# The first 90 microseconds of a decoder layer, reordered: second memory tile, gain row, keys, idle products

## Chip, cores and metric

The kernel runs on one core of a Trainium2 chip. The metric is the device time of one execution, in microseconds. TensorE is called PE, VectorE DVE, ScalarE ACT, GpSimd POOL; SyncE (SP) issues the transfers.

## The reference

One decoder layer on 1024 tokens of width 1024, with 256 memory tokens, everything in float32:

```python
h = rms_norm(x, g_pre_mix);  proj = h @ w_in           # q, k, v, conv gates, qx
q, k = apply_rope(q), apply_rope(k)
y_attn = dilated_mixture_attention(q, k, v)             # 8 heads x 64
y_conv = short_gated_conv(...)
mem_kv = rms_norm(mem, g_mem) @ w_mem_kv                # keys, values of 256 memory tokens
y_x = memory_cross_attention(qx, mem_kv)                # 4 heads x 64
y = concat(rms_norm(y_attn), rms_norm(y_conv), rms_norm(y_x)) @ w_out
x = x + rms_norm(y, g_post_mix)
f = square(relu(rms_norm(x, g_pre_mlp) @ w_up)) @ w_down
x = x + rms_norm(f, g_post_mlp)
```

## The kernel before

Float32 products are made of fp32r parts. `split` copies a value to a high part on ACT (`copy`, L88) and subtracts it for a low part on DVE (`lo_part`, L92). `mm3` (L101 to L103) adds high·high, high·low and low·high into one PSUM bank.

The opening stage stands in one block whose order on ACT, DVE, POOL and PE is written out by hand; SP's order, and all work outside such blocks, is left to a planner. Every engine works through its own queue in order. The stage does the following.

- The memory's gain row (`m_row`) is split on DVE (`spread_row`, L354, L355) and spread over 128 partitions by two products with a row of ones (L357, L358).
- Two memory tiles (`XT[NS]`, `XT[NS+1]`) are squared and summed (`x_sums`, L149 on ACT, L127 on DVE), their reciprocal roots taken on POOL (L130), scaled (`m_norm`, L152), turned by PE (`x_turn`, L304) and split into `mt_h`, `mt_l`.
- The memory weights are cut into parts by `m_cut(k)` into columns of `hh` and `hl` that the tokens need later; ACT makes the high part, and DVE and POOL make the low parts in turn (L364).
- `v_mem(t, k0, k1)` adds the values of memory tile t into a bank, `v_out` takes them out. `k_mem(pr, k0, k1)` and `k_out(pr)` do so for the keys of head pair pr; the keys use the two `mm` banks, which the query products `raw_mms` use after them. `k_out` makes high parts (`KM`), low parts on DVE, and shifted copies (`KMS`).
- The row of `g_pre_mix` is spread by one float32 product per half (`p_spread`, L669), and copied from its bank to `g_tok[0]`.
- Eight token tiles in the order 7 to 0 are squared, normed (`x_norm`, L152), turned and split into `hh`, `hl`. `raw_mms(n, k0)` makes q, k, v of head group 0 for tile n, two of eight chunks at a time. Its weights are cut by `cut` (ACT, L88) and `low` (DVE and POOL in turn, L232).
- `tables` computes the angles in small DVE steps, placed by `table_steps`. `rope0(m)` rotates tile m's q and k on DVE or POOL (L402 to L409). `turn0(c)` turns two tiles by PE (L635) and splits them into `QK` and shifted copies `KS`. The three `qk` tiles are used in rotation, so rope m+3 waits for the turn that reads rope m.
- The weights of head group 1 (`wj1`) are cut in four pairs; the first three projection steps of that group (`steps13`) run in the block, and attention (`pair_windows`) follows.

Of the kernel before, what the change touches and what calls it, by code (L numbers as in the profile page):

```python
# [9 lines left out]
F = mybir.dt.float32  # L10
R = mybir.dt.float32r
# [10 lines left out]
NS = S // 128  # L22
# [23 lines left out]
def hybrid_block(ctx, tc, x, mem, positions, g_pre_mix, g_mem, w_in, w_mem_kv, conv_w, g_attn_out,  # L46
                 g_conv_out, g_xattn_out, w_out, g_post_mix, g_pre_mlp, w_up, w_down, g_post_mlp,
                 ident_in, bias_in, invf_in, out):
    nc = tc.nc
# [22 lines left out]
    def mm_bank(cols=512):  # L72
        return bank("mm", 2, cols)
# [10 lines left out]
    def tp_bank():  # L84
        return bank("tp", 1)

    def copy(o, i, scale=1.0):
        nc.scalar.activation(o, i, AF.Copy, scale=scale)  # L88
# [28 lines left out]
    def rstd(ss, width):  # L117

        n = ss.shape[1]
        ms = small.tile([128, n], F, name="ms", tag="ms")  # L120
        widths = width if isinstance(width, (list, tuple)) else [width] * n
        i = 0
        while i < n:
            k = i
            while k < n and widths[k] == widths[i]:
                k += 1
            nc.vector.tensor_scalar(ms[:, i:k], ss[:, i:k], 1.0 / widths[i], EPS, op0=OP.mult, op1=OP.add)  # L127
            i = k
        r = small.tile([128, n], F, name="rstd", tag="rstd")
        nc.gpsimd.tensor_tensor(r, ms, half_neg.to_broadcast([128, n]), op=OP.pow)  # L130
        return r
# [65 lines left out]
    def load_x(n):  # L197
        XT[n] = stage(name="xt")
        nc.sync.dma_start(XT[n], tokens[n])
# [91 lines left out]
    def x_sums(n):  # L291

        ss = small.tile([128, 1], F, name="ss", tag="ss")
        sumsq(ss, XT[n], 1024)
        RS[n] = rstd(ss, D)

    def x_norm(n):
        norm_to(XT[n], XT[n], g_tok[n // NS], RS[n])

    def x_turn(n, q):  # L300
        t = pt_bank()
        for i in range(4):
            k = 4 * q + i
            nc.tensor.transpose(t[:, i * 128:(i + 1) * 128], XT[n][:, k * 128:(k + 1) * 128], ident)  # L304
        v = t.rearrange("p (k s) -> p k s", k=4)
        if n < NS:
            cl = slice(order[n] * 128, (order[n] + 1) * 128)
            split(hh[:, 4 * q:4 * q + 4, cl], hl[:, 4 * q:4 * q + 4, cl], v)
        else:
            if n == NS:  # L310
                mt_h.append(kv.tile([128, 4, 256], R, name="mth", tag="QK", bufs=NSETS))
                mt_l.append(kv.tile([128, 4, 256], R, name="mtl", tag="QK", bufs=NSETS))
            cl = slice((n - NS) * 128, (n - NS + 1) * 128)
            split(mt_h[q][:, :, cl], mt_l[q][:, :, cl], v)

    RS = {}
    p_row = [kv.tile([128, 512], F, name="g_row", tag="KS", bufs=NSETS) for _ in range(2)]
    for q in range(2):
        nc.scalar.dma_start(p_row[q][:1], g_pre_mix[:, q * 512:(q + 1) * 512])
# [31 lines left out]
    def spread_row(row):  # L351

        hi, lo = (kv.tile([128, 512], R, name="row" + n, tag="V", bufs=NSETS) for n in "hl")
        nc.vector.tensor_copy(hi[:1], row)  # L354
        nc.vector.tensor_sub(lo[:1], row, hi[:1].bitcast(F))  # L355
        b = s_bank()
        nc.tensor.matmul(b, ones[:1], hi[:1], start=True, stop=False)  # L357
        nc.tensor.matmul(b, ones[:1], lo[:1], start=False, stop=True)  # L358
        return b

    def m_cut(k):

        copy(hh[:, k, :512], MW[k])
        (nc.gpsimd if k % 2 else nc.vector).tensor_sub(hl[:, k, :512], MW[k], hh[:, k, :512].bitcast(F))  # L364

    def v_mem(t, k0, k1):
        if k0 == 0:
            MB["v", t] = (ot_bank, tp_bank)[t]()
        for k in range(k0, k1):
            cl = slice(t * 128, (t + 1) * 128)  # L370
            mm3(MB["v", t][:, :256], mt_h[k // 4][:, k % 4, cl], mt_l[k // 4][:, k % 4, cl], hh[:, k, 256:512],
                hl[:, k, 256:512], k == 0, k == KT - 1)
    def v_out(t):
            vm = kv.tile([128, 4, 128], R, name="VM", tag="VM", bufs=2)
            split(vm[:, :, 0:64], vm[:, :, 64:128], MB["v", t][:, :256].rearrange("p (h e) -> p h e", h=4))
            VM.append(vm)
# [261 lines left out]
    def table_steps(n):  # L638
        for _ in range(n):
            next(tab, None)  # L640

    with tc.manual_schedule(engines={ACT, DVE, POOL, PE}):
        def cut(n=1):
            for _ in range(n):
                cuts.pop(0)()

        def low(n=1):
            for _ in range(n):
                lows.pop(0)()

        nc.vector.memset(extra[:1, :128], 1.0)
        nc.vector.tensor_copy(ones[:1], extra[:1, :128])
        gb = [spread_row(m_row[:1, :512])]
        ss = small.tile([128, 2], F, name="ss2", tag="ss2")
        for q in range(2):
            sumsq(ss[:, q:q + 1], XT[NS][:, q * 512:(q + 1) * 512], 512)
        s1 = small.tile([128, 1], F, name="s1", tag="s1")
        nc.vector.tensor_add(s1, ss[:, 0:1], ss[:, 1:2])
        r = rstd(s1, D)
        gb.append(spread_row(m_row[:1, 512:]))  # L660

        def m_norm(n, r):
            for q in range(2):
                cl = slice(q * 512, (q + 1) * 512)
                norm_to(XT[n][:, cl], XT[n][:, cl], gb[q], r)

        def p_spread(q):
            b = mm_bank()
            nc.tensor.matmul(b, extra[:1, :128], p_row[q][:1], start=True, stop=True)  # L669
            return b  # L670
        m_norm(NS, r)
        m_cut(0)
        m_cut(1)
        x_turn(NS, 0)
        x_turn(NS, 1)
        m_cut(2)
        v_mem(0, 0, 2)
        pb = [p_spread(0)]
        m_cut(3)
        v_mem(0, 2, 4)  # L680
        pb.append(p_spread(1))
        x_sums(NS + 1)
        m_cut(4)
        m_norm(NS + 1, RS[NS + 1])
        m_cut(5)
        m_cut(6)
        m_cut(7)
        v_mem(0, 4, 6)
        x_turn(NS + 1, 0)
        x_turn(NS + 1, 1)  # L690
        v_mem(0, 6, 8)
        load_x(3)
        load_x(4)
        g_tok[0] = ac.tile([128, S], F, name="g_pre", tag="bias")
        for q in range(2):
            copy(g_tok[0][:, q * 512:(q + 1) * 512], pb[q])
        x_sums(0)
        cut(2)
        low(2)
        v_out(0)  # L700
        v_mem(1, 0, 8)
        tab = tables()
        x_norm(0)
        table_steps(1)
        k_mem(0, 0, 8)
        v_out(1)
        x_turn(0, 0)
        cut(2)
        low(2)
        x_turn(0, 1)  # L710
        x_sums(1)
        k_mem(1, 0, 4)
        cut(2)
        low(2)
        k_out(0)
        k_mem(1, 4, 8)
        x_norm(1)
        cut(2)
        low(2)
        raw_mms(0, 0)  # L720
        k_out(1)
        x_sums(2)
        table_steps(1)
        raw_mms(0, 2)
        x_turn(1, 0)
        x_norm(2)
        raw_mms(0, 4)
        x_turn(1, 1)
        table_steps(4)
        x_sums(3)  # L730
        raw_mms(0, 6)
        for n in range(1, NS):
            if n + 4 < NS:
                load_x(n + 4)
            if n == 5:
                cuts = []
                wj1 = load_w_in(1, later=cuts, engines=[nc.vector])
            if n == NS - 1:
                bias = ac.tile([128, S], F, name="bias", tag="bias")
                nc.sync.dma_start(bias, bias_in)  # L740
            raw_mms(n, 0)
            if n + 1 < NS:
                x_turn(n + 1, 0)
            else:
                cut(2)
            table_steps(2)
            if n == 5:
                for o in (sin, cos):
                    nc.scalar.activation(o, o, AF.Sin, scale=TWO_PI)
            raw_mms(n, 2)  # L750
            if n + 1 < NS:
                x_turn(n + 1, 1)
            else:
                cut(2)
            if n + 2 < NS:
                x_norm(n + 2)
            if n == 4:
                reduces[0]()
            table_steps(2)
            raw_mms(n, 4)  # L760
            if n + 3 < NS:
                x_sums(n + 3)
            table_steps(2)
            for m in {5: (0, 1), 6: (2, 3), 7: (4, 5, 6)}.get(n, ()):
                rope0(m)
            if n == NS - 1:
                cut(2)
            raw_mms(n, 6)
            if n >= 6:
                turn0(9 - n)  # L770
        turn0(1)
        rope0(7, nc.vector)
        cut(2)
        steps13, turn13 = proj_steps(1, 3, wj1)
        run(steps13[:3])
        turn0(0)
# [901 lines left out]
```

## Time and profile before

| | us |
|---|---|
| median of 3 runs | 1160.62 |
| lowest, highest run | 1157.08, 1161.08 |
| profiled execution | 1158.95 |
| its span | 1157.2 |

The span is the time between the first and the last instruction in the trace; the execution's own time holds 1.75 us more. Times in the rows below are counted from the span's start. An engine's idle time before an instruction is put down to what released it last.

### The profile page before, as it was taken

Reading aid. Unit: us, or ns where it says so; the run is one execution under the profiler, and the core shown is the slowest. Engines: PE = TensorE matmul, PEld = TensorE weight load, DVE = VectorE, ACT = ScalarE, POOL = GpSimd, SP = SyncE. Lnnn points to the kernel's source line nnn. Section 1 sums busy time; section 2 is a strip of 40 time slices with the busy share of each in tenths; the row PEclk is TensorE's granted clock in tenths of the full one; section 3 lists DMA queues with packets and bytes.
Section 4 is the critical chain, followed back from the end, with each engine's and each line's share of the span. In section 5 each row is a group of like instructions: output and inputs, shape, how many; then the busy total and the mean of one; then the engine's idle time right before and its main releaser. Section 6 shows DMA issues by size and latency. Waiting matters only on the chain.

```text
span 1157.2 us, 15949 instructions
## 1 busy us (share of the span) xinstructions
PE 1126.8 (97%) x5785; PEld 961.0 (83%) x5785; DVE 787.5 (68%) x1422; ACT 631.1 (55%) x1202; POOL 82.9 (7%) x107
## 2 busy tenths in 40 slices
PE   8989999999999999999999999999999999999997
PEld 6888989898888878888788888888888888888886
DVE  5888777676757547676876656665695565865776
ACT  5667675666657345655665555555564433433551
POOL 3230020202002021110000000000000000000001
PEclk9999999999999999999999999999999999999999
DMA  8230020100020264333365444544885466432216
GB/s 261 80 100 19 10 61 10 51 5 10 24 74 19 72 198 168 123 133 113 107 197 184 147 137 147 171 146 152 293 298 184 134 220 227 168 105 91 93 36 218
DMA packets 118790, 144.27 MB, mean 125 GB/s; under 512 B 7468, under 2 KB 71604, under 8 KB 118711
## 3 DMA queue, kind: packets, MB, share of 16 engines
q1 hardware_dynamic: 118706, 143.25, 37.6%
q8 instruction: 45, 0.74, 0.3%
q14 instruction: 35, 0.28, 0.1%
q10 hardware_dynamic: 4, 0.00, 0.0%
HBM read 101.28 MB, written 41.94 MB: 124 GB/s over the span
## 4 chain that ended last, share of the span: by engine, by line
PE 85%; DVE 6%; ACT 4%; DMA 2%; issue 1%; POOL 0%; SPq 0%; DVEq 0%; POOLq 0%; ACTq 0%
PE pt L1559 7%; PE sc L1559 7%; PE mm L1559 7%; PE mm L101 6%; PE mm L103 6%; PE mm L102 5%; PE tp L1559 3%; PE ot L1559 3%; PE sc L1263 2%; PE sc L1264 2%; PE sc L1262 2%; PE pt L565 2%; PE mm L1262 2%; PE mm L1264 2%; PE mm L1263 2%; PE sc L500 2%
## 5 line engine op out<-in xcount | busy, mean ns | idle before, releaser
L88 ACT ACTIVATE op<-fraw 128x1024 fp32r<-128x1024 f32 x56 | 59.4, 1060 | 142.2 <-PE tp L1559 72.5
L92 DVE TENSOR_TENSOR op<-fraw,op 128x1024 fp32r<-128x1024 f32 x56 | 68.5, 1224 | 89.3 <-ACT op L88 87.5
L101 PE MATMUL mm<-wh,hh 128*128 128x384 f32 x256 | 91.3, 357 | 4.1 <-DVE KM L92 2.2
L103 PE MATMUL mm<-wh,hl 128*128 128x384 f32 x256 | 87.5, 342 | 0.0
L102 PE MATMUL mm<-wl,hh 128*128 128x384 f32 x256 | 87.3, 341 | 0.0
L1559 PE MATMUL pt<-op 128*128 128x512 f32 x336 | 80.7, 389 | 0.0
L1559 PE MATMUL mm<-op 128*128 128x512 f32 x336 | 80.4, 389 | 0.0
L1559 PE MATMUL sc<-op 128*128 128x512 f32 x336 | 80.4, 389 | 0.0
L1559 PEld LDWEIGHTS pt<-op 128*128 128x128 f32 x336 | 63.1, 188 | 13.1
L1559 PEld LDWEIGHTS mm<-op 128*128 128x128 f32 x336 | 63.1, 188 | 13.1
L1559 PEld LDWEIGHTS sc<-op 128*128 128x128 f32 x336 | 63.1, 188 | 13.1
L92 DVE TENSOR_TENSOR tl<-pt,th 128x512 fp32r<-128x512 f32 (+1 forms) x96 | 59.8, 642 | 13.7 <-ACT th L88 12.8
L92 DVE TENSOR_TENSOR op<-r_b,op 128x1024 fp32r<-128x1024 f32 x56 | 68.3, 1219 | 0.6 <-ACT op L88 0.6
L554 ACT ACTIVATE P<-P,m 128x896 f32<-128x896 f32 (+3 forms) x64 | 49.7, 776 | 30.4 <-DVE m L552 29.7
L1246 ACT ACTIVATE ef<-ef 128x512 f32<-128x512 f32 x48 | 30.3, 631 | 60.4 <-DVE ef L1285 36.0
L144 POOL TENSOR_TENSOR rstd<-ms,half_neg 128x1 f32<-128x1 f32 x24 | 13.5, 561 | 679.7 <-DVE ms L142 679.7
L88 ACT ACTIVATE th<-pt 128x512 fp32r<-128x512 f32 (+1 forms) x96 | 52.1, 560 | 15.0 <-PE pt L565 13.2
L88 ACT ACTIVATE op<-r_b 128x1024 fp32r<-128x1024 f32 x56 | 58.5, 1045 | 3.2 <-issue 3.2
L232 POOL TENSOR_TENSOR wl<-wraw,wh 128x384 fp32r<-128x384 f32 (+1 forms) x40 | 37.4, 963 | 299.4 <-ACT wh L88 253.8
L101 PEld LDWEIGHTS mm<-wh,hh 128*128 128x128 f32 x256 | 49.0, 191 | 4.6 <-issue 2.4
L101 PE MATMUL mm<-hh,wh 128*128 128x512 f32 x128 | 51.9, 405 | 0.0
L103 PE MATMUL mm<-hh,wl 128*128 128x512 f32 x128 | 50.9, 398 | 0.0
(389 smaller groups left out, 3112.3 us busy)
## 6 DMA issues: line engine op xcount, KB each, us to landing
wuraw<-in_w_up SPq DMA_DIRECT2D x32, 512.0 KB, 4.7
f_s<-ef SPq DMA_DIRECT2D x64, 256.0 KB, 2.1
r_b<-in_w_down SPq DMA_DIRECT2D x32, 512.0 KB, 4.8
fraw<-f_s SPq DMA_DIRECT2D x32, 512.0 KB, 3.7
f_a<-ef SPq DMA_DIRECT2D x48, 256.0 KB, 4.0
fraw<-f_a SPq DMA_DIRECT2D x24, 512.0 KB, 4.0
wraw<-in_w_in SPq DMA_DIRECT2D x24, 192.0 KB, 2.7
xt<-in_x SPq DMA_DIRECT2D x8, 512.0 KB, 5.4
```

The lines of the kernel that those rows point to most:

```text
L88: nc.scalar.activation(o, i, AF.Copy, scale=scale)
L92: nc.vector.tensor_sub(lo, src, hi.bitcast(F))
L101: nc.tensor.matmul(o, a_hi, b_hi, start=first, stop=False)
L102: nc.tensor.matmul(o, a_hi, b_lo, start=False, stop=False)
L103: nc.tensor.matmul(o, a_lo, b_hi, start=False, stop=last)
L232: eng.tensor_sub(wt[1][:, :cols], rv[:, k], wt[0][:, :cols].bitcast(F))
L554: nc.scalar.activation(p[:, :nk], p[:, :nk], AF.Exp, scale=-1.0, bias=m, accum_out=den[:, 2 * i + h:2 * i + h + 1])
L1246: nc.scalar.activation(t, t if src is None else src, AF.Relu)
L1262: nc.tensor.matmul(b, w[:, 0, k], th[:, k], start=(k == 0 and not prev), stop=False, skip_group_check=True)
L1263: nc.tensor.matmul(b, w[:, 0, k], tl[:, k], start=False, stop=False, skip_group_check=True)
L1264: nc.tensor.matmul(b, w[:, 1, k], th[:, k], start=False, stop=(k == 3), skip_group_check=True)
L1559: nc.tensor.matmul(b, x[:, k, cl], y[:, k], start=(fresh and s == 0 and k == 0 and m == 0), stop=(s == NSUB - 1 and k == 1 and m == 2), sk ...
```

## The change

A tile of zeros (`zr`) is made on DVE at the start, and `keep` issues products on it into a bank that nothing reads: seven before the first spread row, five between the two, two after them. The second memory tile's square, norm and turn are placed ahead of most of the first tile's value products. The row of `g_pre_mix` is split and spread as the memory's row is, around the first half of the second tile's value products, and the first token tile is normed from the banks. The first keys are taken out before the first token tile is turned; the cuts of the query weights are spread over later places. In the loop over tiles, rope 5 runs on DVE instead of POOL, rope 4 runs one tile earlier, and the last cut of head group 1's weights runs ahead of the turns.

```diff
+    zero = kv.tile([128, 384], F, name="zero", tag="V", bufs=NSETS)
+    zr = kv.tile([128, 384], R, name="zr", tag="V", bufs=NSETS)
+    nc.vector.memset(zero, 0.0)
+    nc.vector.tensor_copy(zr, zero)
+    def keep(src, n, cols=384):
+        b = tp_bank()
+        for _ in range(n):
+            nc.tensor.matmul(b[:, :cols], src[:, :128], src[:, :cols], start=True, stop=True)
...
+        keep(zr, 7)
         gb = [spread_row(m_row[:1, :512])]
...
         r = rstd(s1, D)
+        keep(zr, 5)
         gb.append(spread_row(m_row[:1, 512:]))
...
-        def p_spread(q):
-            b = mm_bank()
-            nc.tensor.matmul(b, extra[:1, :128], p_row[q][:1], start=True, stop=True)
-            return b
+        keep(zr, 2)
         m_norm(NS, r)
         m_cut(0)
         m_cut(1)
         x_turn(NS, 0)
         x_turn(NS, 1)
         m_cut(2)
+        x_sums(NS + 1)
+        m_cut(3)
         v_mem(0, 0, 2)
-        pb = [p_spread(0)]
-        m_cut(3)
+        m_norm(NS + 1, RS[NS + 1])
+        m_cut(4)
+        m_cut(5)
         v_mem(0, 2, 4)
-        pb.append(p_spread(1))
-        x_sums(NS + 1)
-        m_cut(4)
-        m_norm(NS + 1, RS[NS + 1])
-        m_cut(5)
         m_cut(6)
         m_cut(7)
-        v_mem(0, 4, 6)
         x_turn(NS + 1, 0)
         x_turn(NS + 1, 1)
-        v_mem(0, 6, 8)
+        x_sums(0)
+        v_mem(0, 4, 8)
         load_x(3)
         load_x(4)
+        pb = [spread_row(p_row[0][:1])]
+        v_mem(1, 0, 4)
+        pb.append(spread_row(p_row[1][:1]))
+        v_mem(1, 4, 8)
+        v_out(0)
         g_tok[0] = ac.tile([128, S], F, name="g_pre", tag="bias")
         for q in range(2):
-            copy(g_tok[0][:, q * 512:(q + 1) * 512], pb[q])
-        x_sums(0)
-        cut(2)
-        low(2)
-        v_out(0)
-        v_mem(1, 0, 8)
-        tab = tables()
-        x_norm(0)
-        table_steps(1)
+            cl = slice(q * 512, (q + 1) * 512)
+            copy(g_tok[0][:, cl], pb[q])
+            norm_to(XT[0][:, cl], XT[0][:, cl], pb[q], RS[0])
         k_mem(0, 0, 8)
         v_out(1)
-        x_turn(0, 0)
-        cut(2)
-        low(2)
-        x_turn(0, 1)
         x_sums(1)
-        k_mem(1, 0, 4)
         cut(2)
         low(2)
         k_out(0)
+        x_turn(0, 0)
+        k_mem(1, 0, 4)
+        x_turn(0, 1)
+        cut(2)
+        low(2)
         k_mem(1, 4, 8)
         x_norm(1)
+        tab = tables()
+        k_out(1)
+        raw_mms(0, 0)
         cut(2)
         low(2)
-        raw_mms(0, 0)
-        k_out(1)
         x_sums(2)
-        table_steps(1)
+        table_steps(2)
         raw_mms(0, 2)
+        cut(2)
+        low(2)
         x_turn(1, 0)
...
-            for m in {5: (0, 1), 6: (2, 3), 7: (4, 5, 6)}.get(n, ()):
-                rope0(m)
+            for m in {5: (0, 1), 6: (2, 3, 4), 7: (5, 6)}.get(n, ()):
+                rope0(m, nc.vector if m == 5 else None)
             if n == NS - 1:
                 cut(2)
             raw_mms(n, 6)
+            if n == NS - 1:
+                cut(2)
             if n >= 6:
                 turn0(9 - n)
         turn0(1)
         rope0(7, nc.vector)
-        cut(2)
```

## Rows read from the trace of the kernel before

**Rows 1.** The page: busy us, share of the span, instructions.
```profile
PE 1126.8 (97%) x5785; PEld 961.0 (83%) x5785; DVE 787.5 (68%) x1422; ACT 631.1 (55%) x1202; POOL 82.9 (7%) x107
```

**Rows 2.** Busy us (instructions) by stretch; then granted clock, DMA share, GB/s.
```profile
29.90:32.10 2.20, 0.01 (x1) 0.00 (x0) 1.48 (x4) 1.71 (x5) 1.53 (x2) 1.00 0.07 28
32.10:40.30 8.20, 8.16 (x40) 7.57 (x41) 5.03 (x9) 7.43 (x16) 1.54 (x2) 0.79 0.10 20
40.30:60.90 20.60, 20.49 (x130) 19.96 (x130) 19.29 (x45) 11.21 (x25) 2.49 (x4) 1.00 0.33 102
...
87.80:91.40 3.60, 3.60 (x15) 3.54 (x16) 1.92 (x5) 1.71 (x4) 0.00 (x0) 0.53 0.35 104
91.40:112.00 20.60, 19.48 (x147) 18.00 (x145) 17.29 (x52) 15.59 (x30) 0.00 (x0) 1.00 0.01 2
112.00:140.00 28.00, 27.83 (x197) 27.59 (x197) 21.39 (x60) 18.33 (x43) 0.00 (x0) 1.00 0.04 11
```

**Rows 3.** Order of time on PE: start, us, engine, line, operation.
```profile
10.89 2.07 PE L669 MATMUL mm<-g_row,extra 1*128 1x512 f32 x2
...
13.92 0.41 PE L102 MATMUL ot<-hl,mth 128*128 128x256 f32 x1
14.13 0.41 PE L103 MATMUL ot<-hh,mtl 128*128 128x256 f32 x1
...
25.79 0.28 PE L102 MATMUL mm<-mtl,hh 128*128 128x256 f32 x1
25.91 0.28 PE L103 MATMUL mm<-mth,hl 128*128 128x256 f32 x1
...
35.06 0.52 PE L102 MATMUL mm<-wl,hh 128*128 128x384 f32 x1
35.38 0.52 PE L103 MATMUL mm<-wh,hl 128*128 128x384 f32 x1
```

**Rows 4.** What PE waited for, 0 to 130: total us, times, longest.
```profile
PE mm L101 <- DVE KM L92: 2.2, 1, 2.2
PE mm L101 <- ACT wh L88: 1.8, 1, 1.8
PE sc L635 <- POOL qk L409: 1.5, 1, 1.5
PE sc L635 <- DVE qk L409: 1.3, 1, 1.3
```

**Rows 5.** Operations on the gain rows: ns min/median/max, first and last start.
```profile
L354 DVE CAST rowh<-g_row x2: 405/410/414, 4.0 to 5.3; 1x512 fp32r<-1x512 f32 x2
L355 DVE TENSOR_TENSOR rowl<-g_row,rowh x2: 678/679/680, 4.5 to 5.8; 1x512 fp32r<-1x512 f32 x2
```

**Rows 6.** Order of time on ACT.
```profile
30.33 0.76 ACT L88 ACTIVATE KM<-mm 64x256 fp32r<-64x256 f32 x2
...
37.57 1.32 ACT L88 ACTIVATE hh<-pt 128x512 fp32r<-128x512 f32 x2
```

**Rows 7.** Groups by shape, 0 to 92: count, busy us, mean ns, idle before.
```profile
L152 DVE SCALAR_TENSOR_TENSOR xt<-xt,rstd,g_pre 128x1024 f32<-128x1024 f32 x8 | 10.6, 1331 | 0.0
...
L149 ACT ACTIVATE sq<-xt 128x1024 bf16<-128x1024 f32 x9 | 9.5, 1052 | 0.0
...
L364 POOL TENSOR_TENSOR hl<-mraw,hh 128x512 fp32r<-128x512 f32 x4 | 5.6, 1402 | 3.4 <-ACT hh L88 3.4
...
L88 ACT ACTIVATE wh<-P 128x384 fp32r<-128x384 f32 x8 | 3.7, 521 | 0.0
...
L88 ACT ACTIVATE KMS<-KM 64x512 fp32r<-64x512 f32 x4 | 2.5, 629 | 1.0 <-DVE KM L92 1.0
```

**Rows 8.** Order of time on DVE.
```profile
77.80 0.41 DVE L402 TENSOR_TENSOR ra<-qkraw,cos 128x256 f32<-128x256 f32 x1
...
79.11 0.42 DVE L402 TENSOR_TENSOR ra<-qkraw,cos 128x256 f32<-128x256 f32 x1
...
81.76 1.41 DVE L92 TENSOR_TENSOR QK<-sc,QK 64x512 fp32r<-64x512 f32 x2
```

## The prediction

> **What bounds the kernel now.** I read the page first. TensorE (PE) is busy for 97% of the span [rows 1], and from 112 us on for 27.83 of 28.00 us [rows 2]. So whatever the opening stage gives PE sooner reaches the end, and nothing else does. The change touches only the first 92 us. I therefore read that part by stretches, then PE's waits, then the order of time on each engine.
>
> Three losses stand there. First, the opening runs at the lower clock. Two products of 256 columns start 0.21 us apart at 14 us and 0.12 us apart at 25.8 us [rows 3], which is 1.2 and 2.4 GHz, although the granted-clock column reads 1.00 until 32 us. Second, PE stands for 2.2 us from 29.9 to 32.1 [rows 2], waiting for the first keys' low part on DVE, since the query products need that bank [rows 4]. ACT begins to take these keys only at 30.33 [rows 6], although the last product of their sum started before 26 us [rows 3]. After the stand the mean granted clock is 0.79 [rows 2]: products of 384 columns start 0.32 us apart, which is 1.2 GHz [rows 3]. Full speed less 0.21, over 8.2 us, is 1.7 us of clock lost. Third, near 77 to 92 us PE waits 1.5 us for a rope on POOL and 1.3 us for one on DVE, both before the same turn, then 1.8 us for a weight copy [rows 4]; in the 3.6 us after that the mean clock is 0.53 [rows 2], again 1.7 us lost.
>
> Not all of this is PE's to win. From 40.3 to 60.9 DVE is busy for 19.29 of 20.60 us and PE for 20.49 [rows 2], so DVE follows PE closely there.
>
> **Idle products.** Fourteen products of 384 columns on zeros cost PE 14 × 0.32 = 4.5 us at the lower clock [rows 3]. Seven of them (2.2 us) stand before the first gain row, whose conversion starts at 4.0 [rows 5]; PE has nothing before it, so they cost nothing. Without that cover they would cost their 2.2 us. The two DVE writes of the zeros fit before 4.0 too. The other seven stand between the two spread rows and before the first memory tile's turn. A row's parts take DVE 0.41 + 0.68 = 1.09 us [rows 5], and PE needs two products of 0.43 us for them (512 columns at 1.2 GHz), so the free room is some 0.2 us per row. Five products take 1.6 us at the lower clock, 0.85 us at the higher. This delays the first memory tile's second half by 0 to 0.9 us, and ACT's in-order queue passes it on to the second tile. I take 0.3, nearer to zero, because ACT waits for weight loads there anyway.
>
> What a gap does, the rows show: after the 2.2 us stand the clock fell [rows 2]. The new order has such a gap as well, near 11 to 13.5 us, where PE waits for the second tile's norm and has no gain row to run. The Trainium skill (TensorE: Matmul & The Clock Gate, section HAM oscillation) says that gaps between bursts throttle the array again, each time anew; by it the early clock would be lost before most value products, and the idle products would buy nothing. The trace agrees in the gap shown.
>
> **Gain row in fp32r parts.** Removed: two float32 spreads that take PE 2.07 us each [rows 3], 4.1 us. Added: four products of 512 columns, 0.9 us at the higher clock, and on DVE 2 × 1.09 = 2.2 us [rows 5]. The DVE part waits behind the scaling of the first token tile's square sum, which follows that square on ACT (1.05 us [rows 7]); PE's queue holds the second tile's value products behind it. The first tile's norm becomes two halves of the same column count.
>
> **Second memory tile.** Its square moves ahead of one weight copy, its reciprocal root on POOL ahead of one low part (1.40 us [rows 7]), its turn ahead of half the first tile's value products. Estimate: the first value sum ends at 16.5 to 18.3 us, as POOL's low parts allow, and the gain row's parts are ready at 18.3 to 20. Then come 48 products of 0.12 us (second values, first keys), 5.8 us, and the second spread, 0.5. The first key sum ends at 24.6 to 26.5; I take 25.7, against 26.2 before.
>
> **Keys out sooner.** ACT takes the keys at 25.7 instead of 30.33, so the 2.2 us stand goes. What is late next is ACT. From 25.7 its queue holds the key copies (0.76 [rows 6]), a short wait and two shifted copies (0.1 + 1.26 [rows 7]), two turned halves (1.2), two weight copies (1.0 [rows 7]) and the second keys (0.76): 30.8. Their shifted copies wait for DVE, which has a norm of 1.33 us [rows 7] ahead of the low parts, so they start near 31.9. Then 1.26, two weight copies 1.0, a square with its readout 1.25, two weight copies 1.0: the next tile's turned half comes at 36.4, against 37.57 [rows 6], 1.2 us sooner. The 3.9 us of stand and clock are not won in full, because four weight copies now stand behind the second keys. Bounds: −3.9 us if PE sets the pace, +1.5 if these copies come late. Less the 0.3 above, the head gives −0.9; with half of the small gain before the keys, I take −1.2.
>
> **Ropes and last cut.** A rope on DVE costs 1.31 us, from the start of one to the start of the next [rows 8]. Rope 4 moves one tile earlier; rope 5 moves from POOL to DVE, into rope 4's place. So the turn that waited for ropes 4 and 5 still waits for a DVE rope there. Rope 4 now stands ahead of the low parts of the first key turn: these, ACT's shifted copies behind them and the weight copies behind those come 0.9 us later. The turn's wait then ends near 80.1 instead of 79.1: +0.9. The last weight cut moves ahead of two key turns. The 1.8 us wait goes, and 11 of 48 projection products (1.9 us) are done before the last turn instead of behind it; the second fall of the clock may go too (1.7). But the cut's two low parts on DVE, 1.0 us, stand ahead of the key low parts that started at 81.76 [rows 8]; these move by 0.9 + 1.0 = 1.9 us. Through two further key turns and the last rope the last turn moves by the same, less the 0.8 us by which it was late behind the weight wait at half clock: +1.1 for the first attention scores. Bounds: +1.1 if DVE and ACT set the pace behind it, where DVE is busy for 17.29 of 20.60 us; −2.0 if PE does, which has 1.1 us free there [rows 2] and 3.1 us less to do. I take the middle, −0.3, and set +0.3 against it for the stand of 4 us before the turn, after which the clock may fall once more. Tail: 0.
>
> Transfers: none is added, and none moves past another.
>
> **Sum.** −1.2 + 0 on the profiled execution's 1158.95 gives 1157.75. The median of the runs is 1.67 us above that execution and their lowest is below it, so I forecast 1158.0.
>
> **Rivals.** (A) The forecast, −3 to +1: 0.55. (B) PE sets both places: −3.9 and −2.0, so −5.9 and 1153. For it: the waits named are PE's. Against it: DVE's 19.29 of 20.60. A clock that the idle products raise early and that stays up belongs here; the Trainium skill (TensorE: Matmul & The Clock Gate, section What's actually happening) says that activity releases the throttle, which no row of an idle product shows yet. Chance 0.18. (C) The mended waits come back as others in the tail: PE stands from 76 to 80.1, and as after the 2.2 us stand the clock falls, so 1.7 us more; with +1.1 for the scores and −1.2 for the head, +1.6, so 1160.6. For it: the new stand is longer than the one that lowered the clock. Against it: PE runs ahead afterwards. Chance 0.17. (D) Slower: the weight copies for the last half of the first query products come so late that these end after the 40.3 us of before. I place the last low part, on POOL, at 37.3, so 2.6 us more decide. At 5 us, with one more fall of the clock, the head is 4.1 worse than before, the tail adds 1.1: +5, 1164. Chance 0.10.
>
> About 0.5% (5.8 us) is what a measurement of this kernel can tell from no change. Faster by that is half of B and a little of A: 0.12. Slower is nearly half of D and a little of C: 0.05. Same: 0.83. The range 1152 to 1163 leaves out the deep end of B and the far end of D.
>
> **What would show it.** Right: no PE wait for a key's low part, no granted clock below 1 near 33 us, key copies near 26, the turned half near 36.4, the turn near 80 still waiting for a DVE rope, low parts of keys near 83.7 (both less the head's gain). Wrong: PE waiting on weight low parts after 32 us, the gain row holding PE near 17 us for over 2 us, or the clock falling in a new place. If the planner orders the work after 92 us differently, the sum fails for a reason outside it.

## The result, and the profile after

The changed kernel takes 1171.86 us, median of 5 runs (1170.00 to 1173.77); the kernel before takes 1160.62 on the same chip (5 runs, 1157.08 to 1161.08). The ratio is 1.0101, 95% interval 1.0082 to 1.0121: about 1% slower, +11.2 us, outside the range of the prediction. The profiled execution took 1170.0, 11.05 more than that of before. One execution of the last version below took 5906.4 us and is left out of its figures.

The page, PE's line (busy us, share of the span, instructions), which answers to [rows 1]:

```profile
PE 1135.1 (97%) x5799; PEld 970.4 (83%) x5799; DVE 792.8 (68%) x1433; ACT 631.1 (54%) x1202; POOL 80.5 (7%) x103
```

PE still counts 97% busy, but has 8.3 us more of it with only 14 more instructions. Products at the lower clock and idle products both count as busy, so the share hides the loss.

I first asked where the loss arises, by instructions that both kernels have. The table gives their starts in the profiled executions.

| start of | before | after | difference |
|---|---|---|---|
| last product of the first key sum | 25.91 | 28.67 | +2.8 |
| first keys taken out by ACT | 30.33 | 29.00 | −1.3 |
| first query product | 32.14 | 32.52 | +0.4 |
| load of ACT's sine table (behind the opening tiles) | 62.06 | 68.97 | +6.9 |
| load of ACT's exponential table (attention) | 93.52 | 102.96 | +9.4 |
| first product of the last stage | 845.1 | 856.1 | +11.0 |

So 6.9 us are lost by the sine table, 2.5 between it and the exponential table, and 1.6 far behind the change, where a fall of the clock costs 1.7 (last row of the windows below). The first two steps hold three separate causes, and each has its own place below.

**Place 1, 34 to 46 us.** PE's waits from 0 to 130 (total us, times, longest), which answer to [rows 4]:

```profile
PE sc L263 <- DVE extra L261: 6.1, 1, 6.1
PE sc L646 <- DVE qk L420: 4.0, 1, 4.0
PE sc L511 <- DVE QK L92: 2.0, 2, 1.7
...
PE ot L102 <- POOL hl L375: 1.0, 1, 1.0
```

The wait for the keys' low part (2.2) is gone, as forecast. In its place stands one of 6.1 us, for line 261, which no sentence of the prediction mentions. PE in order of time:

```profile
28.67 0.29 PE L103 MATMUL mm<-mth,hl 128*128 128x256 f32 x1
...
32.52 0.33 PE L101 MATMUL mm<-wh,hh 128*128 128x384 f32 x1
...
33.57 0.34 PE L103 MATMUL mm<-wh,hl 128*128 128x384 f32 x1
40.01 0.27 PE L263 MATMUL sc<-ident,extra 8*128 8x8 f32 x1 [6.10 <-DVE extra L261]
...
42.29 1.05 PE L304 MATMUL pt<-ident,xt 128*128 128x128 f32 x4
```

L263 is a turn of 8 by 8 numbers, the positions of the tokens, and the first step of the angle table. It waits for a cast of them on DVE (L261). Behind the wait the clock is at 0.50 until about 44.9 (windows below), which costs another 2.4 us. Before, the cast started at 25.36 on DVE, and PE turned the numbers without a wait:

```profile
33.41 0.27 PE L263 MATMUL sc<-ident,extra 8*128 8x8 f32 x1
```

The change put it behind the square sum of the third token tile, and PE's queue is in order, so all query products stand behind those eight columns. DVE, POOL and ACT in the same stretch; DVE and ACT answer to [rows 8] and [rows 6]:

```profile
33.86 2.02 DVE L152 SCALAR_TENSOR_TENSOR xt<-xt,rstd,g_pre 128x1024 f32<-128x1024 f32 x1
35.91 0.87 DVE L92 TENSOR_TENSOR KM<-mm,KM 64x256 fp32r<-64x256 f32 x2
38.22 0.56 DVE L232 TENSOR_TENSOR wl<-P,wh 128x384 fp32r<-128x384 f32 x1 [1.44 <-ACT wh L88]
39.67 0.15 DVE L127 TENSOR_SCALAR ms<-ss 128x1 f32<-128x1 f32 x1 [0.89 <-ACT sq L149]
39.74 0.20 DVE L261 CAST extra<-pos 8x128 f32<-8x128 int32 x1
```

```profile
33.55 1.25 POOL L232 TENSOR_TENSOR wl<-P,wh 128x384 fp32r<-128x384 f32 x1 [4.02 <-ACT wh L88]
```

```profile
29.00 0.77 ACT L88 ACTIVATE KM<-mm 64x256 fp32r<-64x256 f32 x2 [0.54 <-PE mm L103]
...
36.36 1.28 ACT L88 ACTIVATE KMS<-KM 64x512 fp32r<-64x512 f32 x2 [2.25 <-DVE KM L92]
...
38.51 1.04 ACT L149 ACTIVATE sq<-xt 128x1024 bf16<-128x1024 f32 x1
...
43.38 0.60 ACT L88 ACTIVATE hh<-pt 128x512 fp32r<-128x512 f32 x1 [2.91 <-PE pt L304]
```

Read backwards from PE's 40.01: the cast at 39.74 stands behind `ms` at 39.67, which waits for the square on ACT (38.51). ACT is late because the shifted keys (36.36) waited 2.25 us for their low part, which stood behind a norm on DVE (33.86) that took 2.02 us beside a low part on POOL, instead of the 1.33 of [rows 7]. The next tile's turned half comes at 43.38 (before 37.57, [rows 6]; forecast 36.4).

**Place 2, 5.9 to 9.7 us.** PE at the head, then near 21 us:

```profile
1.74 2.61 PE L326 MATMUL tp<-zr 128*128 128x384 f32 x7 [1.74 <-DVE zr L320]
4.45 0.79 PE L368 MATMUL sc<-rowh,ones 1*128 1x512 f32 x1
...
5.89 1.97 PE L326 MATMUL tp<-zr 128*128 128x384 f32 x5
7.79 0.79 PE L368 MATMUL sc<-rowh,ones 1*128 1x512 f32 x1
...
8.94 1.01 PE L326 MATMUL tp<-zr 128*128 128x384 f32 x2
9.74 1.91 PE L304 MATMUL pt<-ident,xt 128*128 128x128 f32 x8
...
20.60 0.41 PE L103 MATMUL ot<-hh,mtl 128*128 128x256 f32 x1
20.99 0.50 PE L368 MATMUL sc<-rowh,ones 1*128 1x512 f32 x1
...
22.36 0.28 PE L102 MATMUL tp<-hl,mth 128*128 128x256 f32 x1
```

The first spread row starts at 4.45; before, this was 4.49, so the first seven idle products cost nothing, as forecast. The next five take 1.97 us and push the second row to 7.79 (5.80 before). The norm of the tile's second half on DVE waits for that row, after:

```profile
9.04 0.75 DVE L152 SCALAR_TENSOR_TENSOR xt<-xt,rstd,sc 128x512 f32<-128x512 f32 x1 [1.98 <-PE sc L369]
```

and before:

```profile
7.32 0.75 DVE L152 SCALAR_TENSOR_TENSOR xt<-xt,rstd,sc 128x512 f32<-128x512 f32 x1 [0.23 <-PE sc L358]
```

The tile's turn starts at 9.74, not at 7.22: 2.5 us late. Nor did these products raise the clock here: a product of 256 columns still takes 0.41 us at 20.60, and the first sign of the higher clock is the row product of 20.99, which takes 0.50 instead of 0.79. Before, that change came near 19.5.

**Place 3, 83 to 106 us.** The stretches with a lowered clock (length, busy us and instructions of PE, PEld, DVE, ACT, POOL, then granted clock, DMA share, GB/s), to be read against [rows 2]:

```profile
38.50:42.00 3.50, 2.00 (x7) 1.97 (x8) 1.19 (x5) 1.97 (x5) 2.81 (x3) 0.50 0.00 0
42.00:46.00 4.00, 4.00 (x20) 3.87 (x19) 1.88 (x2) 0.99 (x2) 0.00 (x0) 0.64 0.00 0
82.50:87.00 4.50, 0.52 (x6) 0.31 (x5) 3.29 (x9) 4.45 (x12) 0.00 (x0) 0.87 0.25 75
87.00:91.00 4.00, 4.00 (x14) 4.00 (x15) 3.83 (x10) 1.03 (x2) 0.00 (x0) 0.50 0.53 152
91.00:95.00 4.00, 4.00 (x20) 4.00 (x20) 2.02 (x4) 2.98 (x5) 0.00 (x0) 0.80 0.56 159
102.00:106.00 4.00, 4.00 (x20) 3.99 (x20) 2.50 (x8) 3.01 (x5) 0.00 (x0) 0.61 0.02 4
425.00:430.00 5.00, 4.03 (x15) 3.37 (x16) 4.84 (x7) 2.89 (x5) 0.13 (x1) 0.71 0.59 174
```

```profile
86.95 1.09 PE L646 MATMUL sc<-ident,qk 128*128 128x128 f32 x4 [3.98 <-DVE qk L420]
...
98.38 0.60 PE L646 MATMUL sc<-ident,qk 128*128 128x128 f32 x4
```

```profile
89.37 1.01 DVE L232 TENSOR_TENSOR wl<-wraw,wh 128x384 fp32r<-128x384 f32 x2
90.42 1.41 DVE L92 TENSOR_TENSOR QK<-sc,QK 64x512 fp32r<-64x512 f32 x2
...
96.18 0.28 DVE L420 TENSOR_TENSOR qk<-ra,rb 128x128 f32<-128x128 f32 x1
```

The first of the two PE rows is the turn that waited in [rows 4] for ropes on POOL (1.5) and DVE (1.3). Now it waits 4.0 us in one piece, and behind it the clock is at 0.50 until about 92.6: 4.0 × 0.50 + 4.0 × 0.20 = 2.8 us lost. The weight cut's low parts (89.37) stand on DVE ahead of the key low parts (90.42), the last turn starts at 98.38 (before 88.13) although its rope on DVE ended at 96.46, and a second fall follows at 102 to 106, behind a wait of 1.7 us for key low parts. The last window, 425 to 430, is a fall that before does not have: 1.7 us by 5.0 × 0.29 and what is left in the next slices.

### The profile page after: what moved, and what is told of

It is laid out like the page before. It is cut to its first block, busy times and chain, and to the rows that moved or that the text cites. A ratio compares the mean times of both kernels' runs of the same rounds, so it can differ in the third digit from the quotient of the medians.

```text
span 1168.2 us, 15977 instructions
## 1 busy us (share of the span) xinstructions
PE 1135.1 (97%) x5799; PEld 970.4 (83%) x5799; DVE 792.8 (68%) x1433; ACT 631.1 (54%) x1202; POOL 80.5 (7%) x103
## 4 chain that ended last, share of the span: by engine, by line
PE 87%; DVE 5%; ACT 4%; DMA 1%; issue 1%; SPq 0%; POOL 0%; DVEq 0%; POOLq 0%; ACTq 0%
PE mm L101 7%; PE pt L1570 7%; PE sc L1570 7%; PE mm L1570 7%; PE mm L103 6%; PE mm L102 6%; PE tp L1570 3%; PE ot L1570 3%; PE sc L1275 2%; PE sc L1274 2%; PE sc L1273 2%; PE pt L576 2%; PE mm L1273 2%; PE mm L1274 2%; PE mm L1275 2%; PE sc L511 2%
## 5 line engine op out<-in xcount | busy, mean ns | idle before, releaser
L1257 ACT ACTIVATE ef<-ef 128x512 f32<-128x512 f32 x48 | 30.3, 631 | 60.3 <-DVE ef L1296 36.0
L102 PE MATMUL mm<-hl,wh 128*128 128x512 f32 x128 | 51.4, 401 | 0.0
```

The costliest lines, as they stand in the source:

```text
L102: nc.tensor.matmul(o, a_hi, b_lo, start=False, stop=False)
L1257: nc.scalar.activation(t, t if src is None else src, AF.Relu)
```

## The experiments

Theory T, formed from this: three independent losses, namely the angle table's step in PE's queue, the idle products between the rows, and the edits to ropes and last cut. Its first rival: the later weight copies (rival D of the prediction) hold up the head, and the angle step only shows where. Its second: some of the three are harmless, and the new order of memory tile, gain row and keys itself costs. The ratios are to the kernel before on the same chip, 95% interval behind them. The changed kernel has five runs, and each of its versions with one thing put back has four. All runs of these versions lie below all five of the changed kernel, but the sizes of the differences are known only to some 2 us.

**The angle table where it stood.** On the changed kernel; the cast then runs before the keys:

```diff
+        tab = tables()
+        table_steps(1)
         k_mem(0, 0, 8)
...
         x_norm(1)
-        tab = tables()
...
         x_sums(2)
-        table_steps(2)
+        table_steps(1)
```

> The changed kernel with one thing put back: the first step of the angle tables (the cast of the positions on DVE) runs before the first key sum, as before, instead of behind the third token tile's square. Theory 1 (three separate losses: the wait of 6.1 us for that cast, the idle products' 2.5 us, the ropes' and last cut's 2.7 us): the wait of PE at L263 goes, the next bound is the weight low parts that end near 42, so 3.5 to 5 us less than the changed kernel, near 1167.5. Theory 2 (the idle products are the loss, all else only passes them on): under 1 us less, because the same engines are late anyway.

Measured: 1168.47, 1.0067 [1.0045, 1.0088], so 3.4 us less than the changed kernel. In this execution the clock rose only at about 25 us in the head and the keys were taken at 30.51, so I count from there. PE's waits (as above), then ACT in order of time:

```profile
PE sc L646 <- DVE qk L420: 4.0, 1, 4.0
...
PE mm L101 <- ACT wh L88: 1.6, 1, 1.6
```

```profile
30.51 0.77 ACT L88 ACTIVATE KM<-mm 64x256 fp32r<-64x256 f32 x2 [0.54 <-PE mm L103]
...
42.03 1.09 ACT L88 ACTIVATE hh<-pt 128x512 fp32r<-128x512 f32 x2
```

The 6.1 is gone, and a wait of 1.6 us for a weight copy stands in its place. From the keys to the sine table took 31.7 us before, 40.0 after and 36.0 here, so of the 8.2 us lost in that stretch 4.0 are the angle step's and 4.2 are not. ACT goes from the keys to the turned half in 11.5 us; the prediction had 10.7. So T explains half of this stretch. The other half is a remainder, for which the wait of 1.6 us for a weight copy speaks, as rival D has it.

**The idle products taken out.** On the changed kernel:

```diff
-        keep(zr, 7)
...
-        keep(zr, 5)
...
-        keep(zr, 2)
```

> The changed kernel without its fourteen idle products; the zeros are still written. Theory 1: the first memory tile's turn starts 2.5 us sooner, and the angle cast's wait moves along with it, so 2 to 3 us less than the changed kernel, near 1169.4. Theory 2: 6 us less or more, near 1165. A third possibility: the products had brought the clock up, and without them the opening is slower, so no gain.

Measured: 1166.87, 1.0063 [1.0044, 1.0082], 5.0 us less than the changed kernel. The turn of the first memory tile starts at 7.22 again, the keys are taken at 26.61, the sine table is loaded at 66.12 (2.9 sooner). PE in order of time:

```profile
10.13 0.41 PE L101 MATMUL ot<-hh,mth 128*128 128x256 f32 x1
...
11.49 0.28 PE L103 MATMUL ot<-hh,mtl 128*128 128x256 f32 x1
...
16.00 0.41 PE L101 MATMUL ot<-hh,mth 128*128 128x256 f32 x1
16.21 0.41 PE L102 MATMUL ot<-hl,mth 128*128 128x256 f32 x1
```

In this execution without idle products the clock rose sooner, not later: products of 256 columns take 0.41 us at 10.13 and 0.28 at 11.49. It was lost again at about 14.2 (0.50 from there to 17.5), after a wait of 1.14 us for a low part on POOL, and 16.00 to 16.21 shows 0.41 again. Of the 4.2 us between the two profiled executions, 2.9 are won by the sine table; the fall of the clock at 425 to 430, worth 1.7, is not in this one, and is the only other large item.

**The tail edits undone, and the tail edits alone.** The first on the changed kernel, the second on the kernel before:

```diff
-            for m in {5: (0, 1), 6: (2, 3, 4), 7: (5, 6)}.get(n, ()):
-                rope0(m, nc.vector if m == 5 else None)
+            for m in {5: (0, 1), 6: (2, 3), 7: (4, 5, 6)}.get(n, ()):
+                rope0(m)
...
             raw_mms(n, 6)
-            if n == NS - 1:
-                cut(2)
...
         rope0(7, nc.vector)
+        cut(2)
```

> The changed kernel with ropes 4 and 5 and the last weight cut as before. Theory 1: 2 to 4 us less than the changed kernel, near 1169, and no stand of 4 us ahead of the turn. Theory 2: within 1 us of the changed kernel, since PE makes up in the attention windows what it lost there.

> The kernel before with only ropes 4 and 5 and the last weight cut moved. Theory 1: 2 to 4 us slower than before, near 1163.5, with the stand ahead of the turn and a fall of the clock after it. Theory 2: within 1 us of before. My prediction had 0 here.

Measured: undone 1168.40, 1.0072 [1.0054, 1.0090], 3.5 us less than the changed kernel; alone 1162.94, 1.0023 [1.0010, 1.0035], 2.6 us more than before. Alone, the sine table is at 62.53 (+0.5) and the exponential table at 96.19 (+2.7): the loss is in the tail and does not need the late head.

**The two tail edits one by one**, on the kernel before: the last cut ahead of the turns, then the ropes.

> The kernel before with only the last weight cut moved ahead of the two turns. Theory 1: half of the ropes' and cut's 2.2 us, +1 us: its low parts on DVE stand ahead of the keys' low parts. Rival: the wait of 1.8 us for the weight copy was on the path, then 1 to 2 us faster.

> The kernel before with only ropes 4 and 5 moved. Theory 1: +1 us, a stand of 4 us ahead of the turn instead of 2.8 in two parts. Rival: rope 5 on DVE only takes the place of rope 4, so 0.

Measured: the cut 1161.82, 1.0010 [1.0001, 1.0019]; the ropes 1162.32, 1.0018 [1.0009, 1.0027]. With the ropes alone the single wait of 4.0 us before the turn is there; with the cut alone that turn waits as before, but PE waits 2.0 us for key low parts behind it. By the medians each is a small loss, 1.5 and 2.0, together 3.5 where both at once gave 2.6. The profiled execution of the ropes alone is only 0.3 above before: its clock had risen by 12.5 us, and it takes the keys at 28.21, which hides most of the loss.

**Idle products alone**, zeros on the kernel before:

> The kernel before with the fourteen idle products alone, in the same three places. Theory 1 (the five and the two between and behind the spread rows stand in front of the first memory tile's norm and turn): that turn 2 to 2.5 us later, the whole head later by as much, near 1162.7. Rival: they are hidden or raise the clock early, 0 or a gain.

Measured: 1163.25, 1.0028 [1.0017, 1.0038]. Here the profile does not bear out the simple story. The first turn is 2.6 us late as in the changed kernel, but the clock was at 2.4 GHz from about 13 to 16.4, while the two float32 spreads run, which then take 1.12 us each instead of 2.07 [rows 3]. The keys are taken at 30.38, as before, and the exponential table is at 93.42. Up to 391 us PE's products start within 0.1 us of where they did before, so all of its 3.1 us arise behind that, where no edit lies: 1.7 by a fall of the clock near 420 (0.72 over 418 to 424), and 1.0 by more standing of PE. So in this execution the early clock paid for the delay, and the loss in the median is not shown to be the delay's.

**The same products on numbers that are not zero**, on the kernel before: six constants in blocks of 64 columns. The edit against the kernel with idle products alone:

```diff
-    nc.vector.memset(zero, 0.0)
+    for i in range(6):
+        nc.vector.memset(zero[:, 64 * i:64 * i + 64], (1.37, -0.71, 2.93, 0.19, -1.83, 0.57)[i])
```

> The kernel before with the fourteen idle products, on six different non-zero constants in place of zeros. In the profiles of four kernels with idle products on zeros, PE ran almost without a gap from 1.7 to 9.7 us and every product up to there was at 1.2 GHz. Theory Z (products on zeros do not raise the clock): here it rises within the opening, before 7 us, the five products take 0.9 us instead of 1.6, and the head is 1 to 3 us shorter than with zeros. Rival (idle products never raise it, whatever they hold): still 1.2 GHz at 9 us, and as slow as with zeros, +2.9 us.

Measured: 1162.71, 1.0021 [1.0011, 1.0030]. PE in order of time:

```profile
1.78 2.61 PE L327 MATMUL tp<-zr 128*128 128x384 f32 x7 [1.78 <-DVE zr L321]
...
6.28 1.97 PE L327 MATMUL tp<-zr 128*128 128x384 f32 x5
...
13.20 0.41 PE L102 MATMUL ot<-hl,mth 128*128 128x256 f32 x1
13.41 0.41 PE L103 MATMUL ot<-hh,mtl 128*128 128x256 f32 x1
```

At 13.20 and 13.41 the products still start 0.21 us apart, and so until about 22. So the clock stays down without zeros too. Here the early clock did not come, and the keys are taken 2.8 us late, at 33.12. Over all fourteen profiled executions the clock rose by 13 us in one of the five with idle products, and in three of the nine without; the other ten rose between 19.5 and 25. That bears out no benefit of them. In none of the four did the early clock stay: it is at 0.50 again from 14.8 to 18.0 us with the ropes alone and in the last version, from 14.2 to 17.5 without idle products, and from 16.5 to 19.8 with idle products alone.

**All three mended**: the angle table early, no idle products, the tail of before. What stays of the change is the second tile's place, the gain row in parts, and the keys out sooner with the later weight copies.

> The changed kernel with all three put back: angle cast early, no idle products, ropes and last cut as before. What is left of the change is the second tile's earlier turn, the gain row in parts, and the keys out sooner with later weight copies. Theory 1: the first keys are taken near 26.5 instead of 30.3, but the query products of the first tile end no sooner, so 0 to 1 us from the kernel before, near 1160.5. Rival (the keys' bank was the bound, as the wait of 2.2 us before suggests): 3 us or more faster than before.

Measured: 1161.29 (ten runs, 1159.33 to 1166.54), 1.0016 [1.0001, 1.0031], 10.6 us less than the changed kernel. The keys are taken at 26.93, 3.4 us sooner than before, yet the sine table is at 63.32 against 62.06. PE's waits up to 110 us:

```profile
PE mm L101 <- ACT wh L88: 1.8, 2, 1.6
...
PE pt L304 <- DVE xt L152: 1.4, 2, 0.8
```

The longest of the first row, 1.6 us for a weight copy, and 0.6 of the second stand before the sine table, and the clock is at 0.50 from 38 to 40 us. So the keys' bank did not bound the head alone: PE next waits for a copy on ACT. Of the second rival this leaves little: the rest of the change costs about 0.9 us by the medians, at the edge of what these runs tell.

**Weight copies kept early, keys out sooner.** On the kernel before: only the order around the first keys changes.

```diff
-        x_turn(0, 0)
         cut(2)
         low(2)
-        x_turn(0, 1)
         x_sums(1)
+        x_turn(0, 0)
+        k_out(0)
+        x_turn(0, 1)
         k_mem(1, 0, 4)
         cut(2)
         low(2)
-        k_out(0)
         k_mem(1, 4, 8)
```

> The kernel before with one reordering: the second pair of query weight cuts and the first token tile's successor's square run on ACT before the first token tile's turned halves come, in ACT's idle time, and the keys are taken behind the first of these halves. Theory 1 (ACT's queue sets the head): 1 to 2 us faster than before, and the wait of 2.2 us for the keys goes. Rival (DVE follows so closely that nothing reaches the end): 0.

Measured: 1160.91, 1.0003 [0.9994, 1.0012], no difference. The wait for the keys' low part is gone, and waits for the token tile's high part (1.6) and for norms (1.6 up to the sine table, of which 0.8 as before) stand in its place. In the profiled execution the keys are taken at 28.56, 1.8 us sooner, and the sine table is loaded at 63.65, 1.6 later.

**Rope 4 one tile earlier, but behind the first key turn and its low parts**, on the kernel before:

```diff
-            for m in {5: (0, 1), 6: (2, 3), 7: (4, 5, 6)}.get(n, ()):
+            for m in {5: (0, 1), 6: (2, 3), 7: (5, 6)}.get(n, ()):
                 rope0(m)
...
             if n >= 6:
                 turn0(9 - n)
+            if n == 6:
+                rope0(4)
```

> The kernel before with rope 4 alone moved, one tile earlier but behind the first key turn's low parts instead of ahead of them, where DVE idles 1.25 us for a weight copy; rope 5 stays on POOL. Theory 1 (the order on DVE decides the tail, not the number of ropes): 1 to 2 us faster than before. Rival (DVE's place for a rope does not matter, PE makes it up): 0.

Measured: 1158.78, 0.9992 [0.9982, 1.0003], unclear. PE's waits up to 110 us:

```profile
PE mm L101 <- ACT wh L88: 2.0, 1, 2.0
PE sc L635 <- POOL qk L409: 1.4, 1, 1.4
```

Of the two rope waits of [rows 4] only POOL's is left; the wait for the weight copy stays (2.0, before 1.8).

**Both of the last two:**

> Both reorderings of the two kernels before this one. Theory 1: their gains add, 2 to 4 us faster than before. Rival: what the head gives is lost again in the tail or to the clock, as the tail's waits follow the clock's falls.

Measured: 1158.69 (median of ten runs), 0.9988 [0.9979, 0.9997]. It is the only version whose interval lies below 1: 1.4 us faster by the ratio (0.3 to 2.4), which among twelve versions is no sure gain. In the profiled execution the exponential table is loaded at 91.47, 2.1 sooner; but its clock had risen by 12.6 us, as in few others, so that execution flatters it, and I go by the runs.

## Why the prediction was wrong

**The step that failed: "What is late next is ACT"**, in the part on the keys. ACT was late next, but PE met its lateness in a step that the sum did not hold. The sum followed ACT's queue and DVE's norm and low parts to the turned half at 36.4, and never costed `table_steps(2)`, a line of the diff. That line put a turn on PE, ahead of six of the eight query chunks, behind a DVE cast that follows a square on ACT. It cost 3.4 us of the median (put back alone), and 4.0 of the stretch from the keys to the sine table. What is queued behind a waiting instruction was asked of the gain row in fp32r parts and not of this step.

**The weight copies, rival D.** Partly right in kind, wrong in size and place. The mended kernel speaks for them: keys 3.4 us sooner, sine table 1.3 later, and a wait of 1.6 for a weight copy between. But with the copies kept early the sooner keys won nothing either, so that the copies are what cost is argued, not shown. The forecast gave this part of the head −1.2 and D 0.10. Two terms of the forecast were too small: the norm on DVE beside POOL (2.02, not 1.33), and the clock behind PE's new waits, which the sum did not charge.

**Idle products, "I take 0.3", bound 0.9.** The first seven were free, as worked out. The step from "the free room is some 0.2 us per row" to a bound of 0.9 failed: 0.9 is the price of the five products at the higher clock (0.85), and they ran at the lower one, took 1.97 and put off the second row by 2.0. The sum also let ACT's wait for weight loads absorb a delay that reaches the second norm, the turn and the tile's value products one to one. The turn was 2.5 us late, and the last two products, 0.6 us at that clock, were never in the sum. Taking them out gave 5.0 us of the changed kernel's median; in the profiles 2.4 us of it stand by the first keys, 2.9 by the sine table. That the delay is what costs is seen in the changed kernel only, where without the products the clock also rose sooner; idle products alone cost 2.9 by the medians, but their profiled execution lost its time elsewhere.

The prediction used the Trainium skill (TensorE: Matmul & The Clock Gate, section HAM oscillation) for the statement that gaps throttle the array anew. The traces agree: 0.50 behind the stands of 6.1 and 4.0 us. The Trainium skill says on the same page (section What's actually happening) that activity releases the throttle. Here that release came late: PE was occupied from 1.74 us on, with 0.96 as its longest stand, and products ran at 1.2 GHz until about 21 us. Rival B's early clock came with the idle products in one execution of five, for 3.5 us, and did not stay up.

**The tail, "Tail: 0", bounds −2.0 and +1.1.** It cost 2.6 us alone and 3.5 in the changed kernel. The places were right: less the head's 6.9, the turn's wait ended at 80.05 (forecast 80.1) and the key low parts started at 83.5 (83.7). Rival C's fall of the clock came and cost 2.8 us instead of 1.7. The last turn was mis-sized: 98.38 less 6.9 is 91.5, 3.35 later than before instead of 1.1. Its rope had ended on DVE at 96.46, which less 6.9 is only 1.4 later than that turn was before. The other 1.9 it stood on PE behind the 48 projection products. The prediction had counted it as a gain that all of them run ahead of this turn; behind the stand of 4.0 us the first 15 of them ran at the lower clock, so they were not done in time. Then PE waited 1.7 us for key low parts, and the clock fell a second time.

**The sum.** Singly undone, the three give 3.4 + 5.0 + 3.5 = 11.9; together 10.6; so by the medians they overlap by 1.3 and explain all but some 0.7 of the 11.2; neither 1.3 nor 0.7 is clear of the noise of these runs. Rivals C and D of the prediction were both partly true, and it had counted them as alternatives. D with C's fall of the clock, 5 + 1.7 on 1158.95, gives 1165.7, still 4.3 short of the profiled 1170.0: the angle step was in no case.

**Open.** From the exponential table to the last stage, where no edit lies, the profiled executions take from 751.5 (before) to 754.7 us (idle products alone). Those of the changed kernel, of the one with the angles early and of the idle products alone hold a fall of the clock between 419 and 431 us, worth 1.7 us each; the other eleven have none. All three have idle products, but two kernels with them are without the fall, so whether an edit makes it likelier stays open. So does why the clock in the head rises as early as 10.7 us in one execution and as late as 25 in another.

## What to carry to other kernels

When a diff moves a step with a name, list for every engine the instructions that it issues, and for each one what it waits for and which long work its queue holds behind it: here a turn of eight columns in an in-order queue held up PE for 6.1 us. If a wait is taken away, follow the next-latest engine as far as the stage's end before writing down a gain; the keys came 3.4 us sooner and the stage ended later. Work meant only to fill an engine was free here in front of a wait of known length, and delayed what stood behind it in the other two places.

## What the hardware showed unexpectedly

- A PE kept occupied is not yet a PE at 2.4 GHz: fourteen products of 384 columns before 10 us left the clock at 1.2 GHz until 21 us or later in four of five profiled executions.
- Where the clock rises is worth some 2 us in this head: among kernels with the head of before, the keys are taken at 28.2 where it had risen by 12.5, and at 30.3 to 31.5 where it rose at 19.5 to 22.
- The clock was lost at 16.4 us in the kernel with idle products alone, and near 14.7 with the ropes alone and in the last version, with no stand of PE above 0.2 us before it. In all three there had been two float32 spreads of a single row; whether these are the cause was not tried.
- A DVE norm of 1024 columns took 2.02 us beside a POOL low part of 384 (2.03 in the mended kernel), and 1.33 us as a mean over the first 92 us of the kernel before.
